# Eleven pairs of projection blocks as seven half-size products, convolution sums in PSUM, LayerNorm by token block

## The chip, the cores and the metric

The kernel runs on one core of a Trainium2 chip. Its metric is the device time of one execution in microseconds (us), the median of three runs. Five engines take part: TensorE (PE in the profile, its weight loads PEld), VectorE (DVE), ScalarE (ACT), GpSimd (POOL) and SyncE (SP), which issues most of the DMAs. Each engine takes its instructions strictly in the order in which they stand for it, so an instruction that waits holds up all that stand behind it on that engine.

## What is computed

One encoder layer over two batches (prompt and sample) of 512 tokens with 1024 channels, in fp32:

```python
h = rms_norm(x, norm_g)
c_q, c_kv, k_rope, gate_a, conv_in, gate_c, mg_a, mg_c = split_columns(h @ w_in)
attn = latent attention of 8 heads from c_q, c_kv and k_rope
y_a = (attn * silu(gate_a)) @ w_o_attn
u = conv_in[..., :1024] * sigmoid(conv_in[..., 1024:])
u = depthwise_conv(u, 31 taps) + dw_bias
u = silu(layer_norm(u, conv_ln_g, conv_ln_b)) * silu(gate_c)
y_c = u @ w_pw2
out = x + (sigmoid(mg_a) * y_a + sigmoid(mg_c) * y_c) @ w_out
```

## The kernel before, in words

**Layout.** The 1024 tokens of both batches lie along the free axis, channels on the 128 partitions. The normalized input h stands in SBUF as 8 slices of channels (k) by 2 batches (b), each 128x512. TensorE multiplies in fp32r, a format of reduced precision, so each operand is split into a high part and the remainder: `hH`, `hL` for h, `whi`, `wlo` for a weight block. A product is then the sum of three: high by high, low by high, high by low.

**Blocks.** The input projection runs in blocks of 128 output channels. One block (`block_mm`, L223) is 8 slices x 2 batches x 3 = 48 matmuls of 128x512 into one pair of PSUM banks. Each block's weights are loaded by SyncE (`load`, L108), rounded by ScalarE (`whi`, L124), and VectorE subtracts to get `wlo` (L125), two blocks ahead (`prep`, L128; `block`, L236). PSUM has three pairs of banks for blocks (pool `pp`) and two single banks (pool `p1`).

**Order of the blocks.** `cb` and `ca` are the gate and the value of the convolution input, `ma` and `mc` the merge gates, `ga` and `gc` the SiLU gates. For each of 8 groups of channels come `cb`, `ca` and two gate blocks; then four more gates and the eight `gc`. Finished `ma`, `mc` and `ga` gates are written out to DRAM (`gate_out`, L313).

**Convolution.** For each group the 31 taps run on all 1024 tokens at once: the first on ScalarE, with the bias (L250), the other 30 on VectorE, each reading and writing the same SBUF tile (L253):

```python
DVE.scalar_tensor_tensor(yt, u[:, :, i : i + S], dwk[:, j, i : i + 1], yt, op0=ALU.mult, op1=ALU.add)
```

`drain(n)` (L256) emits n taps between blocks and alternates between two groups when two are at hand.

**LayerNorm.** All eight convolved groups stay in SBUF. `ln_tok` (L348) transposes one block of 128 tokens to tokens-by-channels in PSUM, takes mean and variance and writes the normalized `z`; `swish` (L363) transposes one group of channels back, applies SiLU with gain and bias, multiplies by the `gc` gate and splits into `cH` and `cL`. Both are placed between the last gate blocks, each `swish` after a later block than its inputs. Then eight blocks multiply by `w_pw2` (`p`, L408), and latents, attention, output projection and the final product follow.

**Who sets the order.** A scheduler places the instructions on each engine: `tc.high_priority` draws some of them forward, `tc.manual_schedule` fixes a stretch at the start. Tiles of a pool rotate, and a tile's next use waits until its last readers are done.

Of the kernel before, what the change touches and what calls it, by code (L numbers as in the profile page):

```python
# [9 lines left out]
F32 = mybir.dt.float32  # L10
# [33 lines left out]
def encoder_block(tc, xp_d, xs_d, win_d, wkr_d, whd_d, wqr_d, wo_d, wp_d, wout_d, vec_d, dwk_d, rg_d, rc_d, yp_d, ys_d):  # L44
# [28 lines left out]
    wp = open_pool("w", bufs=2, side="left")  # L73
# [22 lines left out]
    spill = {"ma": ma_s, "mc": mc_s, "ga": ga_s}  # L96
# [10 lines left out]

    def load(i):  # L108
        src, n = wjobs[i]
        wraw[i] = wp.tile([P, D], F32, tag="raw", bufs=1, name=f"raw{i}")  # L110
        nc.sync.dma_start(wraw[i][:, :n], src)

    def split(i):
# [10 lines left out]
        nc.scalar.copy(hv, rv)  # L124
        DVE.tensor_sub(lv, rv, f(hv))  # L125
        wdone[i] = (hi, lo)

# [11 lines left out]
    others = [("ma", j) for j in range(6)] + [("mc", j) for j in range(KD)] + [("ga", j) for j in range(KD)]  # L139
    for j in range(KD):  # L140
        for key in [("cb", j), ("ca", j)] + others[2 * j : 2 * j + 2]:
            wjob(*key)
    late = others[2 * KD :]
    for key in late + [("gc", j) for j in range(KD)]:
        wjob(*key)
# [13 lines left out]
    for j in range(2):  # L159
        job(("w", j), wout_d[j])  # L160

# [41 lines left out]

    def evac_x(b, banks, ks):
        for k in ks:
            g = vec[:, V_NG + k : V_NG + k + 1]
            hi = hp.tile([P, S], F32R, name=f"hH{k}_{b}")
            lo = hp.tile([P, S], F32R, name=f"hL{k}_{b}")
            ACT(hi, banks[k], AF.Identity, scale=g)  # L209
            DVE.scalar_tensor_tensor(lo, banks[k], g, f(hi), op0=ALU.mult, op1=ALU.subtract)  # L210
            hH[k, b], hL[k, b] = hi, lo
# [29 lines left out]


# [4 lines left out]
    def conv_ops(j, u):  # L247
        yt = yp.tile([P, 2, S], F32, tag="y", name=f"y{j}")
        y[j] = yt
        ACT(yt, u[:, :, 0:S], AF.Identity, scale=dwk[:, j, 0:1], bias=vec[:, V_DB + j : V_DB + j + 1])  # L250
        yield
        for i in range(1, TAPS):
            DVE.scalar_tensor_tensor(yt, u[:, :, i : i + S], dwk[:, j, i : i + 1], yt, op0=ALU.mult, op1=ALU.add)  # L253
# [17 lines left out]
    load(1)  # L271
    banks = {}
# [6 lines left out]
    with tc.manual_schedule(engines={nc.scalar.engine, nc.vector.engine}):  # L279
# [5 lines left out]
        split(1)  # L285
        norm_x(1)
# [4 lines left out]
    for k in range(0, KD, 2):  # L291
        banks = {kk: x_bank(1, kk) for kk in (k, k + 1)}
        trans_x(1, banks, banks)
        evac_x(1, banks, banks)
    for i in (0, 1):
        block_mm(first[i], i, hh, hl, (1,))
        prep(i + 2)
        if i == 0:
            nc.sync.dma_start(dwk, dwk_d)
    DVE.tensor_mul(gqk, vec[:, V_GQ : V_GQ + 1], vec[:, V_GK : V_GK + 1])  # L300
    close_pool("x")
    yp = open_pool("y", bufs=8, side="left")
    sp = open_pool("s", bufs=9, side="left")
    cv = open_pool("cv", bufs=2, side="left")
    rg = cv.tile([P, 4, RD], F32, name="rg", bufs=1)
    rc = cv.tile([P, 2, 4, RD], F32, name="rc", bufs=1)
    nc.sync.dma_start(rg, rg_d)
    nc.sync.dma_start(rc, rc_d)

    def gate(nm, j, pool, tag):  # L310
        gate_out(nm, j, pool, tag, block(J[nm, j]))

    def gate_out(nm, j, pool, tag, ps):  # L313
        st = pool.tile([P, NT], F32, tag=tag, name=f"st{nm}{j}")
        ACT(st, ps, AF.Silu if nm == "ga" else AF.Sigmoid)
        nc.scalar.dma_start(spill[nm][j], st)

    for j in range(KD):
        ps = flat(first[0]) if j == 0 else block(J["cb", j])
        sig = cv.tile([P, NT], F32, tag="sig", name=f"sig{j}")  # L320
        ACT(sig, ps, AF.Sigmoid)
        drain(8)
        ps = flat(first[1]) if j == 0 else block(J["ca", j])
        u = cv.tile([P, 2, UW], F32, tag="u", name=f"u{j}", bufs=4)
        nc.gpsimd.memset(u[:, :, 0:PAD], 0.0)
        nc.gpsimd.memset(u[:, :, PAD + S : UW], 0.0)
        with tc.high_priority(offset=100):
            DVE.tensor_mul(u[:, :, PAD : PAD + S], half(ps), half(sig))
        waiting.append(conv_ops(j, u))
        drain(8)  # L330
        for key in others[2 * j : 2 * j + 2]:
            gate(*key, sp, "s")
            drain(8)
    for i in range(4):
        nc.gpsimd.tensor_mul(rt[:, i], rc[:, i % 2], rg[:, i].unsqueeze(1).to_broadcast([P, 4, RD]))


    sgc = {}
    z = {}
    cH = {}  # L340
    cL = {}

    def gate_c(j):
        ps = block(J["gc", j])
        sgc[j] = sp.tile([P, NT], F32, tag="s", name=f"sgc{j}")
        ACT(sgc[j], ps, AF.Silu)

    def ln_tok(i):  # L348
        ps = pp.tile([P, D], F32, tag="pp", name=f"yT{i}")
        for j in range(KD):  # L350
            nc.tensor.transpose(ps[:, j * P : (j + 1) * P], flat(y[j])[:, i * P : (i + 1) * P], identf)
# [8 lines left out]
        z[i] = zp.tile([P, D], F32, tag="z", name=f"z{i}", bufs=8)  # L360
        DVE.tensor_scalar(z[i], ps, mv[:, 0:1], rs, op0=ALU.subtract, op1=ALU.mult)

    def swish(j):  # L363
        ps = pp.tile([P, NT], F32, tag="pp", name=f"zT{j}")
        for i in range(8):
            nc.tensor.transpose(ps[:, i * P : (i + 1) * P], z[i][:, j * P : (j + 1) * P], identf)
        zs = zp.tile([P, NT], F32, tag="zs", name=f"zs{j}", bufs=2)
        ACT(zs, ps, AF.Silu, scale=vec[:, V_LG + j : V_LG + j + 1], bias=vec[:, V_LB + j : V_LB + j + 1])
        DVE.tensor_mul(zs, zs, sgc[j])
        cH[j] = yp.tile([P, NT], F32R, tag="y", name=f"cH{j}")  # L370
        cL[j] = sp.tile([P, NT], F32R, tag="s", name=f"cL{j}")
        nc.scalar.copy(cH[j], zs)
        DVE.tensor_sub(cL[j], zs, f(cH[j]))

    for key in late[:2]:
        gate(*key, sp, "s")
        drain(16)
    drain(1000)
    close_pool("cv")
    zp = open_pool("z", bufs=2, side="left")  # L380
    for n, key in enumerate(late[2:]):
        gate(*key, sp, "s")
        if n > 0:
            ln_tok(2 * n - 2)
            ln_tok(2 * n - 1)
    for j in range(KD):
        gate_c(j)
        if j == 0:
            ln_tok(6)
            ln_tok(7)  # L390
        else:
            swish(j - 1)
    swish(7)
    close_pool("z")

# [11 lines left out]
    for j in range(KD):  # L407
        ps = block(J["p", j], lambda k, b: cH[k][:, b * S : (b + 1) * S], lambda k, b: cL[k][:, b * S : (b + 1) * S])  # L408
# [4 lines left out]
    close_pool("m", "s", "y")  # L413
# [529 lines left out]
```

## Time and profile before

| what | value |
|---|---|
| median of 3 runs | 1188.58 us (1185.53 to 1188.98) |
| profiled execution, its own time | 1190.66 us |
| its span in the trace | 1188.9 us |
| PE busy | 1169.9 us, 98% of the span |
| DVE busy | 758.9 us, 64% |
| ACT busy | 399.6 us, 34% |
| POOL busy | 83.4 us, 7% |
| start of the first convolution tap | 50.70 us |
| start of the first LayerNorm transpose | 416.37 us |
| start of the first `p` block | 539.97 us |

The profile is one execution seen by the hardware profiler. Its views group instructions by line and shape (how often, busy time, mean duration), list them in order of time, give each engine's busy share in a stretch, and follow back the chain of work that ended last. "Idle before" is the time that the engine stood still ahead of an instruction, with what ended the wait.

### The profile page before, as it was taken

What the parts mean: (1) busy time and instruction counts of PE and PEld (TensorE: products, weight loads), DVE (VectorE), ACT (ScalarE), POOL (GpSimd) and SP (SyncE); (2) the same over time, 40 slices, a digit from 0 to 9 for tenths busy, and PEclk for the clock granted to TensorE, in tenths of its full rate; (3) what the DMA queues carried; (4) which work ended last, traced back from release to release, by engine and by line L of the source; (5) the groups of instructions that cost most, each with busy time, mean ns of one, the idle gap of its engine ahead of it and who ended that gap; (6) DMA issues with size and microseconds to landing.
All of it is one profiled execution on the core that took longest, in us unless ns stands there. A gap on an engine that the chain in (4) does not pass through costs nothing.

```text
span 1188.9 us, 14723 instructions
## 1 busy us (share of the span) xinstructions
PE 1169.9 (98%) x5988; PEld 992.2 (83%) x5988; DVE 758.9 (64%) x1094; ACT 399.6 (34%) x698; POOL 83.4 (7%) x108
## 2 busy tenths in 40 slices
PE   7999999999999999999999999999999999999998
PEld 5788888888888888888888887899999998888887
DVE  5599999999999854233121453777877889344411
ACT  5412211221122112332001335766676687122200
POOL 3000000000000000000000001322222221000000
PEclk9999999999999999999999999999999999999999
DMA  5122122212222321113442012011010112335432
GB/s 212 37 89 89 53 71 89 71 53 89 71 72 75 103 86 56 36 53 116 150 142 70 24 39 89 30 34 34 26 34 19 36 36 90 101 132 169 165 106 71
DMA packets 27571, 92.71 MB, mean 78 GB/s; under 512 B 3184, under 2 KB 3440, under 8 KB 27504
## 3 DMA queue, kind: packets, MB, share of 16 engines
q1 hardware_dynamic: 23760, 79.19, 19.8%
q10 hardware_dynamic: 3744, 12.58, 3.2%
q8 instruction: 47, 0.77, 0.3%
q14 instruction: 20, 0.16, 0.0%
HBM read 70.79 MB, written 20.97 MB: 77 GB/s over the span
## 4 chain that ended last, share of the span: by engine, by line
PE 94%; ACT 2%; DVE 1%; DMA 1%; POOL 1%; issue 0%; SPq 0%; ACTq 0%; DVEq 0%
PE blk L228 63%; PE po L865 7%; PE pt L632 2%; PE pkv L540 1%; PE pkv L542 1%; PE pkv L541 1%; PE av L642 1%; PE av L643 1%; PE av L644 1%; PE sc L613 1%; PE sc L615 1%; PE sc L614 1%; PE sc L616 1%; PE sc L617 1%; PE pq L569 1%; PE pq L570 1%
## 5 line engine op out<-in xcount | busy, mean ns | idle before, releaser
L228 PE MATMUL blk<-hH,whi 128*128 128x512 f32 x848 | 332.5, 393 | 1.6 <-ACT hH L209 0.7
L228 PE MATMUL blk<-hL,whi 128*128 128x512 f32 x848 | 332.6, 392 | 0.2 <-DVE hL L210 0.2
L253 DVE SCALAR_TENSOR_TENSOR y<-u,dwk,y 128x1024 f32<-128x1024 f32 x240 | 298.6, 1282 | 5.1 <-ACT y L250 1.4
L124 ACT CAST whi<-raw 128x1024 fp32r<-128x1024 f32 (+2 forms) x81 | 83.7, 1033 | 556.3 <-PE blk L228 540.9
L228 PE MATMUL blk<-hH,wlo 128*128 128x512 f32 x848 | 265.2, 391 | 0.3 <-DVE wlo L125 0.2
L228 PEld LDWEIGHTS blk<-hH,whi 128*128 128x128 f32 x848 | 160.0, 189 | 36.4 <-ACT hH L209 1.4
L228 PEld LDWEIGHTS blk<-hH,wlo 128*128 128x128 f32 x848 | 160.0, 189 | 34.1 <-DVE wlo L125 1.1
L228 PEld LDWEIGHTS blk<-hL,whi 128*128 128x128 f32 x848 | 160.1, 189 | 33.9 <-DVE hL L210 1.3
L125 DVE TENSOR_TENSOR wlo<-raw,whi 128x1024 fp32r<-128x1024 f32 (+1 forms) x80 | 96.9, 1211 | 126.6 <-ACT whi L124 126.6
L228 PE MATMUL blk<-a,whi 128*128 128x512 f32 x256 | 68.4, 389 | 0.0
L623 ACT ACTIVATE pr<-sc,nm,sqs 128x512 f32<-128x512 f32 x64 | 51.2, 800 | 28.0 <-DVE nm L621 28.0
L228 PEld LDWEIGHTS blk<-a,whi 128*128 128x128 f32 x256 | 48.0, 188 | 9.9
L410 DVE TENSOR_TENSOR tmc<-blk,smc 128x1024 f32<-128x1024 f32 x8 | 9.8, 1225 | 65.1 <-PE blk L228 65.1
L868 DVE TENSOR_TENSOR o<-po,xr 128x1024 f32<-128x1024 f32 (+1 forms) x9 | 10.0, 1106 | 64.1 <-PE po L865 64.1
L228 PE MATMUL blk<-cL,whi 128*128 128x512 f32 x128 | 49.8, 389 | 0.0
L228 PE MATMUL blk<-cH,whi 128*128 128x512 f32 x128 | 49.8, 390 | 0.0
L620 DVE TENSOR_REDUCE nm<-sc 128x1 f32<-128x512 f32 x64 | 43.7, 684 | 6.6 <-PE sc L617 6.4
L634 DVE TENSOR_TENSOR pt<-pt,pt 128x512 fp32r<-128x512 f32 x64 | 43.4, 682 | 1.0 <-ACT pt L633 0.8
L633 ACT CAST pt<-pt 128x512 fp32r<-128x512 f32 x64 | 38.8, 611 | 7.2 <-PE pt L632 7.1
L228 PE MATMUL blk<-a,wlo 128*128 128x512 f32 x128 | 39.4, 389 | 0.0
L228 PE MATMUL blk<-cH,wlo 128*128 128x512 f32 x128 | 39.4, 389 | 0.0
L632 PE MATMUL pt<-identf,pr 128*128 128x128 f32 x256 | 38.9, 275 | 0.0
(203 smaller groups left out, 1865.4 us busy)
## 6 DMA issues: line engine op xcount, KB each, us to landing
raw<-in_win_dram SPq DMA_DIRECT2D x53, 512.0 KB, 3.7
mc_s<-stmc ACTq DMA_DIRECT2D x8, 512.0 KB, 2.9
ga_s<-stga ACTq DMA_DIRECT2D x8, 512.0 KB, 3.3
raw<-in_wp_dram SPq DMA_DIRECT2D x8, 512.0 KB, 5.0
smc<-mc_s SPq DMA_DIRECT2D x8, 512.0 KB, 4.6
tc_s<-tmc SPq DMA_DIRECT2D x8, 512.0 KB, 2.9
sga<-ga_s SPq DMA_DIRECT2D x16, 256.0 KB, 2.6
raw<-in_wo_dram SPq DMA_DIRECT2D x8, 512.0 KB, 4.2
```

Of the source, the lines that this page charges most:

```text
L124: nc.scalar.copy(hv, rv)
L125: DVE.tensor_sub(lv, rv, f(hv))
L228: mm(ps[:, b], (wlo if wl_ else whi)[:, k], xl(k, b) if xl_ else xh(k, b), start=(k == 0 and wl_ == 0 and xl_ == 0), stop=(k == KD - 1 and ...
L253: DVE.scalar_tensor_tensor(yt, u[:, :, i : i + S], dwk[:, j, i : i + 1], yt, op0=ALU.mult, op1=ALU.add)
L540: mm(ps[:, t2], kh_, kh_w[:, k], start=(k == 0), stop=False)
L541: mm(ps[:, t2], kh_, kl_w[:, k], start=False, stop=False)
L620: DVE.reduce_max(nm, ps, axis=AX.X, negate=True)
L623: ACT(pr, ps, AF.Exp, bias=nm, scale=r["sq"][:, j : j + 1], accum_out=sm)
L632: nc.tensor.transpose(pt[:, kt], pr[:, kt * P : (kt + 1) * P], identf)
L633: nc.scalar.copy(pth[:, :, js], pt)
L634: DVE.tensor_sub(ptl[:, :, js], pt, f(pth[:, :, js]))
L865: mm(ps[:, n], lhs[k][:, ts_], w[k][:, n * S : (n + 1) * S], start=first_, stop=last_)
```

## The change

**Seven products for eight.** Of the blocks, 11 pairs are no longer two times 48 matmuls: `cb` with `ca` for the groups 2 to 7, the eight `gc` in four pairs, and `ga` 0 with 1. A pair is a 2x2 matrix (two blocks by two halves of the 1024 channels) times a 2x2 matrix (two halves by two batches), and is formed from 7 products of half depth with sums and differences before and after. A product has 12 matmuls, so a pair has 84. Sums of the weights (`s1` to `s4`) are made by GpSimd, sums of the input (`t1` to `t4`, and their parts `TH`, `TL`) once at the start by VectorE and GpSimd. After the products VectorE forms the outputs with five operations of 128x512 a pair (`u2`, `v`, and three sums in place in PSUM).

**Weights.** From the fifth block on, the low parts of weight blocks before LayerNorm's end are subtracted by GpSimd. Three raw and three split buffers stand where one and two stood.

**Convolution.** One group at a time; the running sum lies in a PSUM pair (`py`, which takes the two banks of `p1` until after the `p` blocks), the last tap writes to SBUF, and the group goes out to DRAM (`y_s`). The `gc` gates go to DRAM too (`gc_s`).

**LayerNorm.** Token block by token block: the block's 8 groups and its gate are loaded back from DRAM, transposed, normalized, transposed back, and finished, between the last six gate blocks. The weights of the first two `p` blocks are prepared after that.

The core of the diff:

```diff
+def sums(n, i1, i2):
+        s1, s2 = t(1), t(2)
+        nc.gpsimd.tensor_add(s1, r2[:, lo_], r2[:, hi_])
+        nc.gpsimd.tensor_add(s2, r1[:, lo_], s1)
...
+def ensure(m):
...
+                    split(i, nc.gpsimd if i >= 4 else None)
...
+                    for q, src in enumerate(sums(n, i1, i2)):
+                        nc.scalar.copy(hi[:, sl], src)
+                        nc.gpsimd.tensor_sub(lo[:, sl], src, f(hi[:, sl]))
...
+plan = [("cb", 0), ("ca", 0), ("cb", 1), ("ca", 1), ("ma", 0), ("ma", 1)]
...
+plan += twos + singles
+NLN = 6
...
+def combine_x(k, banks):
+        ACT(b22, banks[k + 4], AF.Identity, scale=g2)
+        DVE.scalar_tensor_tensor(t[1], banks[k], g1, xw[k], op0=ALU.mult, op1=ALU.subtract)
+        DVE.scalar_tensor_tensor(t[3], banks[k], g1, b22, op0=ALU.mult, op1=ALU.subtract)
+        nc.gpsimd.tensor_sub(t[2], b22, t[1])
+        nc.gpsimd.tensor_sub(t[4], xw[k + 4], t[2])
...
+        for n in (1, 3, 2, 4):
+            nc.scalar.copy(TH[n, k], t[n])
+            nc.gpsimd.tensor_sub(TL[n, k], t[n], f(TH[n, k]))
...
+def seven(emit):
...
+        product(a, e, 0, quad(0, 0), True)
+            nc.scalar.copy(p_a, a)
+        product(b, e, 1, comb(2), True)
+            DVE.tensor_sub(u2, p_a, b)
+        product(d, e + 1, 0, comb(3), True)
+        drain(2)
+        product(b, e + 1, 1, comb(1), False)
+            DVE.tensor_sub(v, p_a, b)
+            DVE.tensor_sub(b, d, v)
+        product(c, e + 2, 0, quad(1, 1), True)
+            DVE.tensor_add(c, c, v)
+        drain(3)
+        product(a, e + 2, 1, quad(1, 0), False)
+        emit(0, flat(px))
+        product(d, e + 3, 0, comb(4), False)
+            DVE.tensor_sub(d, d, u2)
+        drain(3)
+        emit(1, flat(py_))
...
 def conv_ops(j, u):
-            DVE.scalar_tensor_tensor(yt, u[:, :, i : i + S], dwk[:, j, i : i + 1], yt, op0=ALU.mult, op1=ALU.add)
+        yt = py.tile([P, 2, S], F32, tag="py", name=f"py{j}")
+            src = y[j] if i == 1 else yt
+            out = y[j] if i == TAPS - 1 else yt
+            DVE.scalar_tensor_tensor(out, u[:, :, i : i + S], dwk[:, j, i : i + 1], src, op0=ALU.mult, op1=ALU.add)
+        nc.sync.dma_start(y_s[j], flat(y[j]))
...
-            while len(active) < 2 and waiting:
+            while len(active) < 1 and waiting:
...
+    def load_tok(i):
+            nc.sync.dma_start(ytok[i], y_s[:, :, sl].rearrange("j p t -> p j t"))
+            nc.sync.dma_start(stok[i], gc_s[:, :, sl].rearrange("j p t -> p j t"))
...
+    def swish(i, z):
+        for j in range(KD):
+            ACT(zs[:, j], ps[:, j], AF.Silu, scale=vec[:, V_LG + j : V_LG + j + 1], bias=vec[:, V_LB + j : V_LB + j + 1])
...
+    close_pool("z", "s", "w1")
+    wp = open_pool("w", bufs=2, side="left")
+    prep(J["p", 0])
+    prep(J["p", 1])
```

**Where the instructions now stand.** On VectorE, in the middle of the convolution before the change: `y` of two groups, `u` the product of value and gate, `wlo` the low part of a weight block.

```order
L253 SCALAR_TENSOR_TENSOR y_982<-u_978,dwk,y_982 128x1024 [waits DVE_49] x7
L125 TENSOR_TENSOR wlo_1175<-raw_1172,whi_1174 128x1024 [waits DMAHW0_49,PE_49,Activation_49]
L253 SCALAR_TENSOR_TENSOR y_982<-u_978,dwk,y_982 128x1024 [waits DVE_49] x7
L328 TENSOR_TENSOR u_1242<-blk_1187,sig_1178 128x2x512 [waits PE_49,Activation_49]
L125 TENSOR_TENSOR wlo_1239<-raw_1236,whi_1238 128x1024 [waits DMAHW1_49,Activation_49]
L253 SCALAR_TENSOR_TENSOR y_982<-u_978,dwk,y_982 128x1024 [waits DVE_49]
L253 SCALAR_TENSOR_TENSOR y_1246<-u_1242,dwk,y_1246 128x1024 [waits Activation_49]
L253 SCALAR_TENSOR_TENSOR y_982<-u_978,dwk,y_982 128x1024 [waits DVE_49]
```

Nothing there but `u` waits for TensorE's current block, and nothing that TensorE's next matmuls need is made there but `wlo`. On the same engine after the change, one of the `gc` pairs late in the stage: `py` is the sum in PSUM, L373 writes `u2` (printed as u), L379 `v`, L380, L384 and L391 finish three of the four outputs in PSUM.

```order
L373 TENSOR_TENSOR u_2467<-pa_2466,blky_2465 128x512 [waits PE_49]
L409 SCALAR_TENSOR_TENSOR py_2458<-u_2160,dwk,py_2458 128x1024 [waits DVE_49] x5
L379 TENSOR_TENSOR v_2468<-pa_2466,blky_2465 128x512 [waits PE_49]
L409 SCALAR_TENSOR_TENSOR py_2458<-u_2160,dwk,py_2458 128x1024 [waits DVE_49]
L380 TENSOR_TENSOR blky_2465<-blky_2465,v_2468 128x512 [waits DVE_49]
L384 TENSOR_TENSOR blkx_2464<-blkx_2464,v_2468 128x512
L409 SCALAR_TENSOR_TENSOR py_2458<-u_2160,dwk,py_2458 128x1024 [waits DVE_49] x3
L391 TENSOR_TENSOR blky_2465<-blky_2465,u_2467 128x512 [waits PE_49]
L409 SCALAR_TENSOR_TENSOR py_2458<-u_2160,dwk,py_2458 128x1024 [waits DVE_49]
L409 SCALAR_TENSOR_TENSOR py_2458<-u_2160,dwk,py_2458 128x1024 [waits DVE_49,Pool_49]
L409 SCALAR_TENSOR_TENSOR py_2458<-u_2160,dwk,py_2458 128x1024 [waits DVE_49] x4
L373 TENSOR_TENSOR u_2616<-pa_2615,blky_2614 128x512 [waits PE_49,Activation_49]
```

TensorE's next products of a pair wait for these outputs, the taps stand between them, and each tap follows one that writes the same tile. On TensorE, LayerNorm's first place: before, `yT` is a transposed block of tokens.

```order
L351 MATMUL yT_2690<-identf,y_454 128x128 [waits Activation_49]
L351 MATMUL yT_2690<-identf,y_718 128x128
...
L351 MATMUL yT_2709<-identf,y_454 128x128 [waits Activation_49]
...
L228 MATMUL blk_2728<-hH_0_183,whi_2625 128x512
```

After the change, with `zT` the way back to channels and `blki` the next gate block:

```order
L528 MATMUL yT_3352<-identf,yt_3286 128x128 [waits DMAHW2_49,Activation_49]
L528 MATMUL yT_3352<-identf,yt_3286 128x128 x7
L528 MATMUL yT_3371<-identf,yt_3290 128x128 [waits DMAHW4_49,Activation_49]
L528 MATMUL yT_3371<-identf,yt_3290 128x128 x7
L544 MATMUL zT_3390<-identf,z_3369 128x128 [waits DVE_49,Activation_49]
L544 MATMUL zT_3390<-identf,z_3369 128x128 x7
L528 MATMUL yT_3415<-identf,yt_3411 128x128 [waits DMAHW6_49,PE_49]
L528 MATMUL yT_3415<-identf,yt_3411 128x128 x7
L325 MATMUL blki_3440<-hH_0_216,whi_3211 128x512 [waits DVE_49,PE_49]
```

The way back of the first token block, which needs VectorE's `z`, now stands right behind the second block's transposes and ahead of the next gate block.

More of the change, by code (lines that the diff above doesn't have):

```diff
@@ new lines, in encoder_block @@
+    take("cb", 0, flat(first[0]))
+    take("ca", 0, flat(first[1]))
+    for u in plan[2 : len(plan) - NLN]:
+        if isinstance(u[0], str):
+            take(*u, single())
+            drain(8)
+        else:
+            seven(lambda q, ps: take(*u[q], ps))
+            drain(6)
+    drain(1000)
+    close_pool("st", "y", "cv", "py")
+    close_pool("hT")
+    cp2 = open_pool("c", bufs=1, side="right")
+    cH = [cp2.tile([P, KD, S], F32R, name=f"cH{b}") for b in range(2)]
+    cL = [cp2.tile([P, KD, S], F32R, name=f"cL{b}") for b in range(2)]
@@ L307, in encoder_block @@
+    zp = open_pool("z", bufs=2, side="left")
+    rg = zp.tile([P, 4, RD], F32, name="rg", bufs=1)
+    rc = zp.tile([P, 2, 4, RD], F32, name="rc", bufs=1)
     nc.sync.dma_start(rg, rg_d)
     nc.sync.dma_start(rc, rc_d)
[L310 to L333, printed above, removed]
@@ L359, in ln_tok @@
         rsqrt(rs, rs)
[L360 to L394, printed above, removed]
+        z = zp.tile([P, D], F32, tag="z", name=f"z{i}")
```

224 lines of the change are left out of this document (188 added, 36 removed).

## The prediction

> **What bounds the kernel now.** I read the page's busy shares first, then the chain that ended last, then the busy time by stretches of the span, and last the groups of instructions and single engines in order of time. The shares:
>
> ```profile
> PE 1169.9 (98%) x5988; PEld 992.2 (83%) x5988; DVE 758.9 (64%) x1094; ACT 399.6 (34%) x698; POOL 83.4 (7%) x108
> ```
>
> The chain (start, length, what) and three stretches (length, then busy time and count of PE, PEld, DVE, ACT, POOL, then PE's granted clock):
>
> ```profile
> 47.05 369.32 PE blk L228 x1628
> ```
>
> ```profile
> 100.00:200.00 100.00, 100.00 (x443) 82.80 (x442) 93.58 (x77) 20.08 (x20) 0.54 (x6) 1.00 0.23 74
> ```
>
> ```profile
> 47.05:416.37 369.32, 369.32 (x1630) 305.78 (x1631) 344.87 (x282) 72.55 (x71) 0.72 (x8) 1.00 0.24 77
> 416.37:539.97 123.60, 123.60 (x610) 103.56 (x607) 49.72 (x63) 34.31 (x35) 4.26 (x8) 1.00 0.17 56
> ```
>
> TensorE is the bound: nothing else lies on the chain for 369 us, at full granted clock. But VectorE is a close second there, busy 344.87 of 369.32 us, 93%. The page's 64% hides that. A change that takes work from TensorE in this stage has only 7% before VectorE is the bound.
>
> One matmul of 128x512 costs 100/443 = 0.2257 us, a block of 48 costs 10.83 us, a pair of blocks 21.67 us, and a pair of 84 matmuls 18.96 us.
>
> **What TensorE saves.** 11 pairs times 12 matmuls are 132 fewer, at 0.2257: **-29.8 us**. The number of LayerNorm transposes stays at 128.
>
> **What VectorE has to do in the stage of the pairs.** Taps before, first by group, then in order of time (start, length):
>
> ```profile
> L253 DVE SCALAR_TENSOR_TENSOR y<-u,dwk,y 128x1024 f32<-128x1024 f32 x240 | 298.6, 1282 | 5.1 <-ACT y L250 1.4
> ```
>
> ```profile
> 53.03 6.56 DVE L253 SCALAR_TENSOR_TENSOR y<-u,dwk,y 128x1024 f32<-128x1024 f32 x5
> 59.51 1.22 DVE L125 TENSOR_TENSOR wlo<-raw,whi 128x1024 fp32r<-128x1024 f32 x1
> 60.65 9.20 DVE L253 SCALAR_TENSOR_TENSOR y<-u,dwk,y 128x1024 f32<-128x1024 f32 x7
> ...
> 309.96 9.65 DVE L253 SCALAR_TENSOR_TENSOR y<-u,dwk,y 128x1024 f32<-128x1024 f32 x8
> ```
>
> At 60.65 only one group is at hand, so each tap waits for the one before it: (9.20 - 1.28) / 6 = 1.32 us from start to start. At 309.96 two groups alternate: (9.65 - 1.28) / 7 = 1.196 us. The difference of 0.124 us is what the dependence costs. A tap followed by something else takes 59.51 - 53.03 - 4 x 1.32 = 1.20 us, and a two-operand 128x1024 operation 60.65 - 59.51 = 1.14 us. After the change one group runs at a time, so the dependent price is back everywhere. A 128x512 operation comes from LayerNorm's statistics, four in a row up to the next start: (420.58 - 418.18) / 4 = 0.60 us.
>
> ```profile
> 418.18 2.48 DVE L356 BATCH_NORM_STATS2 bst<-yT 128x6 f32<-128x512 f32 x4
> 420.58 0.32 DVE L357 BATCH_NORM_AGGREGATE mv<-bst 128x2 f32<-128x12 f32 x2
> 420.82 0.27 DVE L358 TENSOR_SCALAR lrs<-mv 128x1 f32<-128x1 f32 x2
> 421.69 2.60 DVE L361 TENSOR_SCALAR z<-yT,mv,lrs 128x1024 f32<-128x1024 f32 x2 [0.59 <-POOL lrs L178]
> ```
>
> In the new order VectorE has, from the first `u2` (L373) to the last sum into `c` (L384), 149 taps followed by a tap, 48 followed by something else, 53 half operations and 6 products `u`: 149 x 1.32 + 48 x 1.20 + 53 x 0.60 + 6 x 1.14 = 292.9 us. TensorE has between the same points 1188 matmuls, 268.1 us. VectorE issues in order, `u2` and `v` stand behind taps, and the next products need the PSUM banks that these operations finish. So the longer one sets the pace: 292.9 + 0.7 (the last sum itself and its hand-over) - 268.1 = **+25.7 us**. For a pair that follows a pair, with 15 taps (11 followed by a tap) and 5 halves, this is 22.3 us against 18.96. The weights' `wlo` no longer stand on VectorE there; without their move it would be worse. Behind the last pair only 11 taps are left beside seven blocks (about 70 us), so the end of the convolution costs nothing.
>
> **The unknown in that price: a tap that reads and writes its sum in PSUM.** No row of before writes PSUM from VectorE. The nearest that read it:
>
> ```profile
> L410 DVE TENSOR_TENSOR tmc<-blk,smc 128x1024 f32<-128x1024 f32 x8 | 9.8, 1225 | 65.1 <-PE blk L228 65.1
> L369 DVE TENSOR_TENSOR zs<-zs,sgc 128x1024 f32<-128x1024 f32 x8 | 9.7, 1225 | 5.6 <-ACT zs L368 5.6
> L361 DVE TENSOR_SCALAR z<-yT,mv,lrs 128x1024 f32<-128x1024 f32 x8 | 10.4, 1340 | 2.3 <-POOL lrs L178 2.3
> ```
>
> L410 reads PSUM and L369 does not: 1225 ns both. So I take the old 1282. Bounds: 1225 (-57 ns on 197 taps, -11.2 us) and 1340, L361, which reads PSUM with two per-partition operands (+58 ns, +11.4 us). The dependence could also vanish, 149 x 0.124 = -18.5 us, for a result may be seen sooner in PSUM. Each 0.01 us on a tap is 2.0 us on the kernel while VectorE sets the pace.
>
> [...]
>
> **GpSimd's share.** Its rate on such tiles:
>
> ```profile
> L564 POOL TENSOR_TENSOR kk<-krs,kk 128x512 fp32r<-128x512 f32 x16 | 20.5, 1284 | 40.2 <-ACT kk L562 40.2
> ```
>
> A pair needs 4 sums and 7 low parts: 11 x 1.284 = 14.1 us, under the 18.96, so nothing is added while no other engine stretches these operations.
>
> **The start.** The first gates wait for the sums of the input:
>
> ```profile
> 30.32 1.27 ACT L209 ACTIVATE hH<-xT,vec 128x512 fp32r<-128x512 f32 x2 [3.28 <-PE xT L202]
> ...
> 45.76 1.28 ACT L321 ACT_TABLE_LOAD   x1
> 47.05 1.02 ACT L321 ACTIVATE sig<-blk 128x1024 f32<-128x1024 f32 x1
> ```
>
> ```profile
> L210 DVE SCALAR_TENSOR_TENSOR hL<-xT,vec,hH 128x512 fp32r<-128x512 f32 x16 | 11.6, 748 | 10.9 <-ACT hH L209 10.8
> L605 ACT CAST k<-pkr 128x512 fp32r<-128x512 f32 x16 | 9.8, 613 | 0.0
> L124 ACT CAST whi<-raw 128x1024 fp32r<-128x1024 f32 x71 | 74.7, 1053 | 523.9 <-PE blk L228 518.1 <-PE blk L699 3.4 <-PE pq L570 2.3
> ```
>
> From 30.32, one more weight cast (1.05), the activation (0.64), `t[1]` and `t[3]` (0.75 each), a cast (0.61) and 0.4 of hand-overs put GpSimd's first `TL` at 34.5. ScalarE's cast of the last combined slice stands ahead of the first sigmoid and waits for GpSimd's 20th operation: 34.5 + 20 x 1.284 = 60.2. Then cast 0.61, table load 1.28, sigmoid 1.02: 63.1. That sigmoid frees the PSUM pair for the fourth block, which before started 44 matmuls after 47.05, at 57.0. TensorE waits **+6.0 us**; 3 if some of the 20 fall ahead of the wait, 10 if GpSimd is a sixth slower.
>
> **LayerNorm.** Transposes of before, 16 in one piece of the chain, and one row for a 128x128 activation:
>
> ```profile
> 416.37 1.75 PE yT L351 x16
> ```
>
> ```profile
> 989.03 1.14 ACT L579 ACTIVATE ks<-pkv,rk 128x128 f32<-128x128 f32 x4
> ```
>
> Eight transposes take 0.87 us. At the first place `zT` stands right behind the second block's transposes. Before, the first `z` was done at 421.69 + 1.30 = 422.99, 4.8 us after the transposes began to be read; it can begin one block (0.87) earlier: TensorE waits 4.0. At the next three places TensorE has 3 x 0.87 = 2.6 us of transposes, while ScalarE has sigmoid 1.02, table load 1.28 and eight activations (a little under 1.14 / 4 each as they overlap, 2.1) before the pair of banks comes free: 4.4 - 2.6 = 1.8 each, 5.4. At the last place `zT` waits for `z` of the block just transposed: statistics 1.20, 0.16, 0.13, GpSimd's root 0.6, `z` 1.30, less one other `zT`: 2.5. The first `p` block waits for a weight cast that stands behind the last gate's sigmoid, 1.02 + 1.05, and then for `wlo`, 1.22 less four matmuls: 2.4. Together 14.3. Before, the stretch from 416.37 lost 123.6 - 10 x 10.83 - 16 x 0.87 = 1.3 to the same. So **+13.0 us**, with nothing else to cover it, since all else waits for TensorE; 6 if the scheduler's hand-overs overlap better. The reloads of tokens (8 + 8 of 512 KB) lie a block ahead on SyncE, whose queue holds only weights for later blocks behind them: nothing.
>
> **The sum.** 1190.7 (the profiled execution's own time) + 6.0 - 29.8 + 25.7 + 13.0 = 1205.6; that execution lies 2.1 above the median of its runs, so the forecast is **1203.5 us**.
>
> **The rivals.**
>
> *Taps in PSUM are cheaper and TensorE stays the bound.* If a dependent tap costs 1.20 or less, VectorE's 292.9 falls by 149 x 0.12 = 17.9 and with a duration nearer to L410's by up to 11.2 more: the 25.7 are gone, 1203.5 - 25.7 = **1178 us**. From a price 0.076 us lower on (14.9 us / 197) the change is a gain. For it speaks L410's 1225; against it, that the 0.124 are seen on this very operation. This is the rival on the other side.
>
> *Taps in PSUM are dearer*, as L361: 1203.5 + 11.4 = **1215 us**.
>
> *GpSimd is stretched by VectorE.* The same tiny operation, alone and beside a VectorE run:
>
> ```profile
> 26.13 0.55 POOL L178 TENSOR_TENSOR rr<-rr,mhalf 128x1 f32<-128x1 f32 x1 [0.63 <-DVE rr L191]
> 27.31 1.30 POOL L178 TENSOR_TENSOR rr<-rr,mhalf 128x1 f32<-128x1 f32 x1 [0.64 <-DVE rr L191]
> ```
>
> ```profile
> 27.16 2.74 DVE L197 TENSOR_SCALAR xt<-xt,rr 128x1024 f32<-128x1024 f32 x4
> ```
>
> It took 0.75 us longer there. On all 20 operations at the start this is +15: **1218 us**. In the pairs 11 x 2.03 = 22.4 us would only equal VectorE's 22.3. Against it: at the start VectorE is idle most of the time. [...]
>
> *Start and LayerNorm are hidden*, VectorE being the bound as forecast: 1203.5 - 6.0 - 13.0 = **1184.5 us**. Against it: the new order puts each waiting instruction directly ahead of TensorE's next block.
>
> **How the numbers follow.** Forecast 0.44 (own range 1190 to 1213: tap at L410's duration 1192, the start 3 to 10, LayerNorm 6 to 13), cheaper taps 0.30, dearer taps 0.11, start and LayerNorm hidden 0.08, GpSimd stretched 0.07. Cheaper taps at 1178 less half of what LayerNorm adds give the low end, 1174; the high end, 1220, takes in the dearer taps and the stretched GpSimd. A measurement can tell 0.3%, 3.6 us, from no change. Faster by more: cheaper taps (0.27 of their 0.30) and 0.05 of the hidden start, 0.32. Within: 0.03 + 0.03 + 0.05 of the forecast's lower part, 0.11. Slower: 0.57.
>
> **What would show it.** In the changed kernel's profile: the taps at L409, 1282 ns and 1.32 from start to start (right), or near 1.20 (the first rival); idle time of TensorE ahead of the products L353 to L355, ended by VectorE, about 2.3 us a pair; the first sigmoid at about 62 and TensorE's wait behind it; 128x512 rows of GpSimd near 1284 ns, or near 2000; idle time of TensorE at `zT` and behind it, about 14 us between the first transpose (416.37 before) and the first `p` block. The forecast is wrong if TensorE shows no wait in the pairs, or if its matmuls are no longer 0.2257 apart.

## The result, and the profile after

The changed kernel takes 1245.68 us (median of 4 runs, 1243.87 to 1251.86), the kernel before beside it 1187.05: a ratio of 1.0503, 95% interval 1.0460 to 1.0546. The forecast was 1203.5 us and at most 1220. The direction was right; the loss over before was some four times the forecast.

The page's shares of the changed kernel (its profiled execution took 1251.86 us, span 1250.1):

```profile
PE 1171.0 (94%) x5856; PEld 976.2 (78%) x5856; DVE 772.4 (62%) x1115; ACT 479.3 (38%) x860; POOL 330.7 (26%) x281
```

TensorE has 132 matmuls fewer and is busy as long as before. The stages: the pairs (from the first `u2` to the last sum into `c`), the single blocks behind them, LayerNorm (columns as in the prediction):

```profile
102.00:417.10 315.10, 281.77 (x1168) 219.07 (x1166) 292.73 (x257) 95.05 (x125) 161.11 (x128) 0.98 0.24 81
427.50:498.50 71.00, 71.00 (x316) 58.76 (x315) 15.49 (x13) 15.60 (x16) 20.57 (x12) 1.00 0.50 161
498.50:598.20 99.70, 77.89 (x368) 64.76 (x366) 42.23 (x57) 53.71 (x92) 11.36 (x11) 0.91 0.33 102
```

VectorE is busy 292.73 us in the pairs, forecast 292.9. But the stretch lasts 315.1, so even VectorE idles there, 7%.

The forecast counted 1188 matmuls between the same points; the row has 1168, because the scheduler put some of the last pair's products behind them (the trace has all 5856 of the kernel's matmuls, 5988 less 132). They are worth 1168 x 0.2257 = 263.6 us, so 51.5 are lost. (By the code's count of 1188 it is 47.0, the figure that some expectations below use.) Of the 51.5 us 33.3 are idle. The other 18.2 are mostly restarts: from 152.45 to 153.70 in the rows below two matmuls take 1.25 us, 0.53 of them idle and 0.45 their usual time, so a wait costs some 0.27 us beyond its idle time. Most of the rest is a lower rate behind three of the waits (last section).

What TensorE waited for in the pairs, up to 407 us (in all, times, longest), then in LayerNorm:

```profile
PE blkx L355 <- POOL olo L179: 11.0, 14, 1.4
PE blkx L353 <- ACT ohi L178: 7.4, 14, 0.5
PE blky L353 <- DVE u L373: 6.4, 6, 1.9
PE blki L325 <- ACT whi L128: 2.9, 3, 1.0
PE blki L325 <- POOL wlo L129: 2.5, 2, 1.3
```

```profile
PE blki L325 <- ACT zs L547: 9.4, 3, 3.5
PE zT L544 <- DVE z L538: 7.2, 2, 4.1
PE blk L325 <- ACT whi L128: 2.6, 1, 2.6
PE zT L544 <- ACT stmc L473: 1.3, 1, 1.3
PE yT L528 <- ACT stmc L473: 1.3, 1, 1.3
```

In the pairs most waits are short, and they end with weight parts (`ohi`, `olo`), not with VectorE. One of them on ScalarE and on TensorE:

```profile
152.69 0.62 ACT L178 CAST ohi<-raw 128x512 fp32r<-128x512 f32 x1 [7.54 <-PE blky L354]
```

```profile
152.45 0.39 PE L355 MATMUL blky<-tH,olo 128*128 128x512 f32 x1
153.37 0.50 PE L353 MATMUL blkx<-hH,ohi 128*128 128x512 f32 x1 [0.53 <-ACT ohi L178]
153.70 0.40 PE L354 MATMUL blkx<-hL,ohi 128*128 128x512 f32 x1
154.73 0.50 PE L355 MATMUL blkx<-hH,olo 128*128 128x512 f32 x1 [0.63 <-POOL olo L179]
```

ScalarE had stood still for 7.54 us. It cast as soon as TensorE's product `b'` had freed the weight tile, and TensorE's next product was the one that needed this cast. The order on TensorE, here where a pair follows a pair, shows why. `blkx` holds a and c, `blky` d and b; the number behind `ohi` is the weight tile of the pair (0: a, b; 1: d, b'; 2: c, a'; 3: d'), and only each product's first row is shown:

```
L353 MATMUL blkx_1294<-hH_0_216,ohi_0_1216 128x512 [waits Activation_49]
...
L353 MATMUL blky_1143<-tH_0_373,ohi_3_1181 128x512 [waits DVE_49]
...
L353 MATMUL blkx_1142<-hH_0_232,ohi_2_1147 128x512 [waits DVE_49]
...
L353 MATMUL blkx_1294<-hH_1_359,ohi_2_1299 128x512 [waits Activation_49]
...
L353 MATMUL blky_1295<-tH_0_128,ohi_0_1216 128x512 [waits Activation_49]
...
L353 MATMUL blky_1295<-tH_0_132,ohi_1_1258 128x512 [waits DVE_49]
```

The code has a, b, d, b', c, a', d'. The scheduler runs a, then the previous pair's d' and a', then c, b, d and b'. So c comes ahead of b, and d, ahead of which `u2` must be ready, directly behind b. Seven of the eleven pairs follow a pair; the trace has one wait for `u2` and two places with a wait for weight parts (`ohi`, then `olo`) for each of the seven (the last `u2` at 408.35, behind the window of the table).

### The profile page after: what moved, and what is told of

Its sections match the earlier page's. It is cut to its first block, busy times and chain, and to the rows that moved or that the text cites. A ratio compares the mean times of both kernels' runs of the same rounds, so it can differ in the third digit from the quotient of the medians.

```text
span 1250.1 us, 14992 instructions
## 1 busy us (share of the span) xinstructions
PE 1171.0 (94%) x5856; PEld 976.2 (78%) x5856; DVE 772.4 (62%) x1115; ACT 479.3 (38%) x860; POOL 330.7 (26%) x281
## 4 chain that ended last, share of the span: by engine, by line
PE 61%; ACT 3%; DVE 1%; POOL 1%; issue 0%; ACTq 0%; DVEq 0%; POOLq 0%
PE blk L325 20%; PE blki L325 11%; PE po L1052 7%; PE pt L819 2%; PE pkv L727 1%; PE pkv L728 1%; PE pkv L729 1%; PE av L829 1%; PE av L830 1%; PE av L831 1%; PE sc L803 1%; PE sc L800 1%; PE sc L802 1%; PE sc L801 1%; PE sc L804 1%; PE pq L756 1%
## 5 line engine op out<-in xcount | busy, mean ns | idle before, releaser
L409 DVE SCALAR_TENSOR_TENSOR py<-u,dwk,py 128x1024 f32<-128x1024 f32 x224 | 288.6, 1288 | 6.7
L128 ACT CAST whi<-raw 128x1024 fp32r<-128x1024 f32 (+3 forms) x59 | 60.4, 1024 | 320.7 <-PE blk L325 166.3
L325 PE MATMUL blki<-hH,whi 128*128 128x512 f32 x352 | 141.3, 401 | 14.9 <-ACT zs L547 9.4
L325 PE MATMUL blki<-hL,whi 128*128 128x512 f32 x352 | 139.9, 398 | 0.0
L325 PE MATMUL blki<-hH,wlo 128*128 128x512 f32 x352 | 111.3, 397 | 4.2 <-POOL wlo L129 3.8
L325 PEld LDWEIGHTS blki<-hH,whi 128*128 128x128 f32 x352 | 68.2, 194 | 31.9 <-ACT zs L547 10.1
L179 POOL TENSOR_TENSOR olo<-s,ohi 128x512 fp32r<-128x512 f32 x44 | 58.7, 1345 | 75.9 <-ACT ohi L178 75.9
L353 PE MATMUL blky<-tH,ohi 128*128 128x512 f32 x176 | 70.2, 399 | 7.7 <-DVE u L373 7.2
L355 PE MATMUL blky<-tH,olo 128*128 128x512 f32 x176 | 69.2, 393 | 0.0
L354 PE MATMUL blky<-tL,ohi 128*128 128x512 f32 x176 | 69.1, 393 | 0.0
L325 PE MATMUL blk<-hH,whi 128*128 128x512 f32 x144 | 57.9, 408 | 0.9 <-ACT hH L306 0.7
L325 PE MATMUL blk<-hL,whi 128*128 128x512 f32 x144 | 58.2, 404 | 0.2 <-DVE hL L307 0.2
```

The costliest lines, as they stand in the source:

```text
L179: nc.gpsimd.tensor_sub(lo[:, sl], src, f(hi[:, sl]))
L325: mm(ps[:, b], (wlo if wl_ else whi)[:, k], xl(k, b) if xl_ else xh(k, b), start=(k == 0 and wl_ == 0 and xl_ == 0), stop=(k == KD - 1 and ...
L353: mm(ps, hi[:, k], xh, start=first and k == 0, stop=False, skip_group_check=not first)
L354: mm(ps, hi[:, k], xl, start=False, stop=False, skip_group_check=not first)
L355: mm(ps, lo[:, k], xh, start=False, stop=k == 3, skip_group_check=not first)
L409: DVE.scalar_tensor_tensor(out, u[:, :, i : i + S], dwk[:, j, i : i + 1], src, op0=ALU.mult, op1=ALU.add)
```

## The experiments

Each ratio is to the kernel before on the same chip, with its 95% interval. That kernel's medians went from 1187.05 to 1190.08 us, so a difference of up to some 3 us between two of the kernels below is not settled.

**Half the taps.** In `conv_ops`:

```diff
+            if i % 2 == 0 and i != TAPS - 1:
+                yield
+                continue
```

> Leaves out 14 of each group's 30 VectorE taps (the even ones but the last), in the same places of the order, so the convolution is not computed in full; everything else stays. In the changed kernel VectorE is busy 292.7 of the 315.1 us between the first u2 and the last sum into c, and TensorE has 268.1 us of matmuls there. Theory A (VectorE's taps set the pace of the pairs): 112 taps of 1.3 us go, TensorE becomes the bound, and the stretch falls by 30 to 45 us: 1200 to 1215 us. Theory B (weights set the pace: of TensorE's idle time in that stretch 23.8 us end with ScalarE's or GpSimd's weight parts, 6.8 us with VectorE): only those 6.8 us go, 1235 to 1240 us. Both in part: about 1220 us, with the weights' waits of some 20 us still in the trace.

1240.25 us, 1.0433 (1.0415 to 1.0452): 5 us less. The stretch with VectorE at little more than half:

```profile
102.00:417.00 315.00, 286.84 (x1202) 226.72 (x1201) 176.36 (x165) 98.55 (x128) 164.14 (x130) 0.98 0.25 86
```

TensorE still idles for 28 us. Theory A, the forecast's own, falls. The waits for weight parts did not stay at 18.4 us either: leaving out taps changes what the scheduler lays out, and 9.0 were left, with 9.5 us behind the sigmoids of three pairs in their place. The time lies 0.25 us above B's range; its reason came out only in part.

**A fourth weight buffer.** In `split` and `ensure`, every fourth weight tile from a pool of its own:

```diff
+        q = wx if wx is not None and len(made) % 4 == 3 and len(made) < len(stream) - NLN else wp
-        hi = wp.tile([P, D], F32R, tag="whi", name=f"whi{i}")
+        hi = q.tile([P, D], F32R, tag="whi", name=f"whi{i}")
```

> A fourth buffer for the split weights (high and low part) in the stage of the pairs; to make room the rotary tables are made behind LayerNorm. Nothing is left out. Theory B (TensorE waits because a cast can begin only when the third buffer back is free, directly ahead of its use): the waits on ScalarE's and GpSimd's weight parts, 23.8 us, go almost wholly, and the time falls by 15 to 22 us to 1224 to 1230 us. Theory A (VectorE sets the pace): TensorE waits for VectorE in their place, at most 5 us are gained: 1240 us or more, with TensorE's idle time ended by VectorE risen from 6.8 to about 25 us.

1225.01 us, 1.0304 (1.0286 to 1.0321): 20.7 us less, as B has it.

**No pairs.**

```diff
     plan += twos + singles
+    plan = [k for u in plan for k in ([u] if isinstance(u[0], str) else list(u))]
```

> No pair is formed from seven products: every block is 48 matmuls again; taps in PSUM, one group at a time, 8 to a block, weights on GpSimd and LayerNorm by token block stay as in the changed kernel. 132 more matmuls are 29.8 us. Theory A: 8 taps take 10.6 us beside a block of 10.83, so VectorE no longer holds TensorE and the 47 us lost in the pairs go: 1246 + 29.8 - 47 = about 1228 us. Theory B: a block's weights are needed as closely as before, 10 to 20 us of waits remain: 1238 to 1250 us. If the loss does not come from the pairs at all: 1275 us.

1226.80 us, 1.0315 (1.0300 to 1.0331). TensorE was busy in all 315 us of the old stretch. So without any pair the change costs 37 us (start and LayerNorm), and the eleven pairs, which take away 29.8 us of matmuls, make the kernel 19 us longer instead. A's number came out, but at eight taps a block nothing there tells VectorE from the order of the products.

**SiLU gates at the end.**

```diff
-    singles = [("ga", j) for j in range(2, KD)] + [("ma", j) for j in range(2, 6)] + [("mc", j) for j in range(KD)]
+    singles = [("ma", j) for j in range(2, 6)] + [("mc", j) for j in range(KD)] + [("ga", j) for j in range(2, KD)]
```

> The six gate blocks that stand between the token blocks of LayerNorm are ga gates (SiLU, as LayerNorm's own activation) in place of mc gates (sigmoid), so that ScalarE loads no activation table there; the order of the gates is all that changes. Theory L1 (ScalarE's chain of weight cast, table load, gate, table load and eight activations of 0.35 us is what TensorE waits for at three places): 2.6 us less at two places and 1.3 to 2.6 at the third and at the last, 7 to 12 us faster: 1234 to 1239 us. Theory L2 (the stage is slow by its granted clock of 0.91 and by waits for z, which do not depend on tables): less than 3 us faster.

1234.81 us, 1.0385 (1.0364 to 1.0407): 10.9 us less, within L1's range.

**Four buffers and half the taps**, both edits as above.

> Four split buffers and, of each group's 30 VectorE taps, 14 left out (the convolution is not computed in full). With three buffers leaving out the taps gave 5 us, with all taps the fourth buffer gave 21 us, and with it TensorE still loses about 28 us to the pairs (1225.0 us, of which 37.3 us over before are seen without any pair). Theory A2 (once the weights come in time, VectorE's 293 us of work set the pace, the term of the forecast): the time falls by 20 to 28 us to 1197 to 1205 us. Theory C (each pair loses by its hand-overs on ScalarE: copies, gates and casts that wait in order): it falls by less than 8 us, 1217 us or more.

1222.89 us, 1.0285 (1.0248 to 1.0322): 2.1 us less than with all taps, no more than the noise. A2 falls. With VectorE busy 177 us of the 315, the waits in the pairs are:

```profile
PE blky L355 <- DVE u L375: 5.7, 5, 1.5
PE blkx L355 <- ACT ohi L180: 4.8, 9, 0.6
PE blkx L357 <- POOL olo L181: 3.1, 5, 0.6
PE blky L355 <- DVE blky L382: 2.1, 3, 0.9
```

The fourth buffer did not end the waits for weight parts: 7.9 us are left. As much, 7.8 us, ends with VectorE, although it has less to do. That it begins only when TensorE is already waiting fits this, but this run alone does not show it.

**LayerNorm staggered**, with four buffers and SiLU gates at the end; `l` is a token block's transposes and `z`, `s` the way back, one list behind each gate block, and a token block's reload follows its transposes:

```diff
-    NLN = 6
+    NLN = 9
+    steps = [["l0", "l1"], ["s0", "l2"], ["s1", "l3"], ["s2", "l4"], ["s3", "l5"], ["s4", "l6"], ["s5", "s6", "l7"], ["s7"], []]
```

> Four split buffers; ga gates (SiLU) and three mc gates as the last nine blocks; and LayerNorm staggered: a token block goes back to channels only behind the next gate block, so that nothing TensorE needs is made directly ahead of it. Nothing is left out. Theory L1 (LayerNorm's 30 us are waits of TensorE for a chain directly ahead of it, the lower clock following from them): 22 to 28 us less than with four buffers alone, 1197 to 1203 us, and a granted clock of 1.0 in that stage. Theory L2 (the stage's clock and reloads from DRAM set its time): 1210 us or more.

1207.52 us, 1.0157 (1.0126 to 1.0187): 17.5 us less, between L1 and L2. TensorE now came to LayerNorm so early that it waited 8.8 us for the reload of a group whose convolution had just ended; without that it would be L1's number, which no run shows.

**The same without pairs.**

> No pairs (every block 48 matmuls), the late gates and the staggered LayerNorm as in the run beside it. By L1 1226.8 - 25 = 1202 us. With the pairs and four buffers 28 of the 29.8 us that they save are lost again, so the two should come out within 4 us of each other; if the pairs are a clear gain by now, this one is slower by more than 8 us.

1203.19 us, 1.0119 (1.0084 to 1.0154): 23.6 us less than the other kernel without pairs. It is 4.3 less than the kernel with pairs, but the two intervals overlap. The granted clock of its profiled execution is 1.00. L1 holds.

**Four taps a group off VectorE**, in the staggered kernel with pairs. `ahead` does the first four taps of the groups 1 to 7, one group early:

```diff
+            ACT(tmp, u[:, :, i : i + S], AF.Identity, scale=dwk[:, j, i : i + 1])
+            nc.gpsimd.tensor_add(y[j], y[j], tmp)
```

> As the kernel with four buffers and staggered LayerNorm, and of the groups 1 to 7 four taps each leave VectorE: ScalarE multiplies, GpSimd adds, one group ahead. VectorE is relieved of 28 x 1.32 = 37 us. Theory A2 (VectorE sets the pace of the pairs once the weights come in time): 18 to 26 us less than without it, 1174 to 1184 us, faster than before the change. Theory C: no gain, or a loss where the additions (28 x 2.4 us on GpSimd) delay the weights.

1204.80 us, 1.0133 (1.0106 to 1.0159): 2.7 us less, with overlapping intervals. A2 fails a second time.

**The products in another order**, in the changed kernel; the weights are made in that order too, and the taps' places between the products move along:

```diff
-            stream += [(n, i, i + 1) for n in range(4)]
+            stream += [(n, i, i + 1) for n in (0, 2, 1, 3)]
...
-        product(d, e + 1, 0, comb(3), True)
+        product(c, e + 1, 0, quad(1, 1), True)
         drain(2)
-        product(b, e + 1, 1, comb(1), False)
+        product(a, e + 1, 1, quad(1, 0), False)
+        ensure(e + 5)
+        product(d, e + 2, 0, comb(3), True)
+        drain(3)
+        product(b, e + 2, 1, comb(1), False)
...
-        product(c, e + 2, 0, quad(1, 1), True)
...
-        drain(3)
-        product(a, e + 2, 1, quad(1, 0), False)
```

> The changed kernel with one thing moved: the seven products of a pair stand as a, b, c, a', d, b', d', and their weights are made in that order, so that c and a' (5.4 us) lie between b and the products that wait for u2, and each weight tile is used by two products in a row. Three split buffers and all taps stay. Theory C (TensorE loses by what is made directly ahead of its use: weights that were needed out of their order, and u2): most of the 18.4 us of waits for weight parts of the pairs and the 7.2 us for u2 go, 15 to 25 us faster: 1221 to 1231 us. Theory A (VectorE's 293 us): VectorE is left as busy, at most 5 us: 1241 us or more. If the number of buffers and not the order is the cause: less than 8 us.

1202.93 us, 1.0105 (1.0088 to 1.0122): 42.8 us less than the changed kernel, far beyond what any theory gave. The same stretch:

```profile
102.00:417.10 315.10, 315.10 (x1387) 259.46 (x1386) 295.51 (x261) 107.81 (x137) 172.67 (x134) 1.00 0.29 99
```

TensorE is never idle, with VectorE at 295.51 us as before and the same three weight buffers.

**The order of products alone**, the weights made in the old order:

> The changed kernel with the products of a pair in the order a, b, c, a', d, b', d', but with their weights still made in the old order, so that c and a' use the third weight tile ahead of the second. Theory W (weights needed out of the order in which they are made are what TensorE waited for): the waits for weight parts stay, 12 to 18 us, only u2's 7 us go: 1225 to 1238 us. Theory H (what counts is that c and a' lie between b and the products that wait for u2 and v): 1203 to 1210 us, as with both moved.

1206.46 us, 1.0147 (1.0130 to 1.0165): theory H. In its trace no wait for weight parts is left in the pairs. The cast that stood directly ahead of its product now starts two products early, when a' frees a tile:

```profile
148.10 0.62 ACT L178 CAST ohi<-raw 128x512 fp32r<-128x512 f32 x1 [4.82 <-PE blkx L354]
```

**Everything together**: the order of products, four buffers, staggered LayerNorm and four taps off VectorE; then with the first sigmoid drawn forward (`tc.high_priority(offset=1500)` around the first two `take`); then with the fourth block's low part on GpSimd (`i >= 3` for `i >= 4`).

> The order of products a, b, c, a', d, b', d' in the kernel with four split buffers, staggered LayerNorm and four taps a group on ScalarE and GpSimd (1204.8 us). Theory C: of its 14 us of waits in the pairs 8 to 12 go, and the half rate behind the longer ones: 1190 to 1197 us. If VectorE set the pace there, no gain: 1202 us or more.

1186.14 us (10 runs, 1175.96 to 1187.79), 0.9944 (0.9916 to 0.9971): faster than before the change, and below the range that theory C gave.

> As the kernel beside it, with the first sigmoid drawn ahead of ScalarE's cast that waits for GpSimd's sum of the input. If that cast holds TensorE (the 1.8 us ahead of the fourth block) the kernel gains 2 to 3 us against the one beside it; if the sums hold TensorE elsewhere, nothing.

1180.85 us (1177.76 to 1186.07), 0.9922 (0.9892 to 0.9952), the lowest median of all. The two sets of times overlap, so the 2 to 3 us are not settled. TensorE waited 10.4 us for the sigmoid in the profiled execution of the kernel beside it (1187.79 us) and 2.5 us in this one's (1177.76 us), but that difference does not lie in the cast that the edit moved: in the profile of the kernel beside it this cast took 0.61 us and waited for nothing. In both, VectorE's `wlo`, then a load of weights, then ScalarE's cast of them come ahead of the sigmoid; first the kernel beside it, then this one:

```profile
55.82 8.78 DVE L130 TENSOR_TENSOR wlo<-raw,whi 128x1024 fp32r<-128x1024 f32 x1 [1.33 <-ACT whi L129]
68.11 0.62 ACT L180 CAST ohi<-raw 128x512 fp32r<-128x512 f32 x1 [10.34 <-DMA raw<-in_win_dram]
```

```profile
55.02 1.46 DVE L130 TENSOR_TENSOR wlo<-raw,whi 128x1024 fp32r<-128x1024 f32 x1 [1.36 <-ACT whi L129]
59.98 0.62 ACT L180 CAST ohi<-raw 128x512 fp32r<-128x512 f32 x1 [3.01 <-DMA raw<-in_win_dram]
```

SyncE issued that load at 64.63 and at 56.52, each time as soon as `wlo` had let go of the raw weights, so the 8.78 us of `wlo` (last section) delayed the sigmoid. Behind the first 100 us of the one and the first 90 of the other, both executions take 1086 us.

> The fastest kernel so far (1180.9 us, runs of 1177.8 to 1186.1) with the low part of the fourth block's weights on GpSimd in place of VectorE, where it took 8.8 us in seven of the runs before it, locked out from its start to the first gap in GpSimd's row of operations. If that lock-out makes the spread of the runs at the start, all runs come near the low end: 1175 to 1180 us. If the spread comes from elsewhere, the median stays at 1180 to 1184 us.

1183.88 us (6 runs, 1181.64 to 1186.35), 0.9952 (0.9935 to 0.9969): no gain. The lock-out was not gone, it had moved to the first tap (last section). Whether the times of the runs that were not profiled spread by the same chain stays open, and so does the share of each edit in the sum: the new order with the staggered LayerNorm alone was not run.

## Why the prediction was wrong

**The matmuls.** 132 fewer at 0.2257 us: right, -29.8 (the traces have 5988 and 5856); with the order mended TensorE shows 0.2272 (315.10 / 1387 recorded).

**VectorE's work.** Right to the microsecond: 292.73 busy, 292.9 forecast, though partly by terms that cancel. The seven first taps, which read their sum from SBUF, took 1718 ns on average, 3.0 us more than forecast in all. The taps with their sum in PSUM:

```profile
L409 DVE SCALAR_TENSOR_TENSOR py<-u,dwk,py 128x1024 f32<-128x1024 f32 x224 | 288.6, 1288 | 6.7
```

```profile
77.89 23.87 DVE L409 SCALAR_TENSOR_TENSOR py<-u,dwk,py 128x1024 f32<-128x1024 f32 x18
```

1288 ns each, (23.87 - 1.29) / 17 = 1.33 us from start to start. The two rivals on the price of a tap are both out: 1288 against 1282 ns. GpSimd's 128x512 rows took 1345 ns (`olo`) and not 2000, so that rival is out as well; and the start and LayerNorm were not hidden, as the next terms show.

**The step that failed** is "So the longer one sets the pace: ... = +25.7 us" (its own terms add up to 25.5). Pace was the wrong measure. GpSimd's share, "so nothing is added", rests on the same comparison of sums, and 18.4 us of TensorE's waits ended with the weight parts `ohi` and `olo`. TensorE needs from VectorE only five short operations a pair, and `u` in six pairs, not the taps; the taps may fall behind, since the blocks after the pairs need nothing of them. Nor, in the main, did the taps hold up `u2`:

```profile
L373 DVE TENSOR_TENSOR u<-pa,blky 128x512 f32<-128x512 f32 x11 | 7.5, 686 | 8.7 <-PE blky L355 8.7
```

In nine of the eleven pairs VectorE stood idle, 8.7 us in all, until TensorE's product b was there. TensorE in turn waited 7.2 us for `u2`, 0.7 a pair where the forecast's sign was 2.3. How much room there was shows in the first LayerNorm row of the changed kernel:

```profile
499.40 2.49 DVE L533 BATCH_NORM_STATS2 bst<-yT 128x6 f32<-128x512 f32 x4 [56.06 <-PE yT L528]
```

VectorE had been done for 56 us. In the kernel with the new order the last tap starts at 436.57 (442.06 in the changed kernel), so VectorE hardly changes, while the first transpose starts at 449.6, not at 498.5. What cost the 51.5 us was, nearly all of it, the order: where a pair follows a pair, each of a, c and d stood directly behind the product that freed its weight tile or on which its `u2` waited. A wait of about 1 us each, with a restart behind it, and the lower rate behind some. Moving c and a' between b and d returned 42.8 us: in the same stretch some 2 us were then lost (315.1 less 1387 x 0.2257), and 4.8 came back as a wait for reloaded tokens, as LayerNorm began earlier. TensorE's order as built held the clue; the prediction read VectorE's order for the pairs, and TensorE's only for LayerNorm.

**LayerNorm.** Forecast 14.3 us of waits, measured 21.8; with the matmuls at 240 x 0.2257 + 128 x 0.109 = 68.2, the 99.7 us lost 31.5. The first place was right (4.0 forecast, 4.1 measured), the last (2.5 against 3.1) and the first `p` block (2.4 against 2.6) nearly so. At the places between, the forecast had gate, one table load and eight activations, 4.4 us. The trace:

```profile
519.69 1.06 ACT L128 CAST whi<-raw 128x1024 fp32r<-128x1024 f32 x1 [8.13 <-PE blki L325]
520.76 1.28 ACT L473 ACT_TABLE_LOAD   x1
522.06 1.02 ACT L473 ACTIVATE stmc<-blki 128x1024 f32<-128x1024 f32 x1
523.10 1.28 ACT L547 ACT_TABLE_LOAD   x1
...
544.87 2.90 ACT L547 ACTIVATE zs<-zT,vec 128x128 f32<-128x128 f32 x8
```

A weight cast and a second table load stand ahead of the gate, and eight activations take 2.90, not 2.1: 7.5 us in a row, so 9.4 + 2.6 us of waits for 5.4. The SiLU gates took 10.9 us of this away. The other 9.7 us of the 31.5 are restarts and slow matmuls, which the forecast did not have.

**The start.** Forecast 6.0. TensorE's matmuls in the first 100 us, before and after:

```profile
0.00:50.00 50.00, 40.53 (x177) 30.68 (x178) 23.75 (x41) 26.85 (x39) 9.19 (x26) 1.00 0.37 137
50.00:100.00 50.00, 50.00 (x222) 41.40 (x221) 47.57 (x39) 9.88 (x10) 0.00 (x0) 1.00 0.23 74
```

```profile
0.00:50.00 50.00, 38.01 (x161) 27.52 (x162) 28.26 (x46) 30.66 (x49) 33.01 (x35) 1.00 0.40 150
50.00:100.00 50.00, 47.78 (x210) 38.95 (x209) 42.84 (x28) 18.62 (x24) 33.03 (x30) 1.00 0.14 51
```

399 against 371: 28 x 0.2257 = 6.3 us. The first sigmoid started at 61.71, forecast about 62: it stood on ScalarE behind a cast that waited 2.25 us for GpSimd's `t` and began at 59.78, though TensorE had ended the sigmoid's own block by 55.13. The fourth block behind it started at 62.79, forecast 63.1. But TensorE came to that block at 61.0, not at 57.0 as forecast, so the wait there was 1.8 us. The rest was lost ahead of it, largely in short waits that the forecast did not have; that 6.0 and 6.3 agree so closely is partly luck.

**The sum in the two profiled executions**, 61.2 us of span: 6.3 - 29.8 + 51.5 + 30.2 (31.5 less the 1.3 that before lost) + 3.0 behind LayerNorm = 61.2. With the order of products mended the kernel takes 1202.9, the forecast's number by other terms, which is luck.

## What to carry to other kernels

When two engines exchange small results and one may run ahead, the larger busy sum need not set the pace; look at each exchange for what stands between the producer's start and the consumer's first instruction, in the order as built. Half the load taken from a suspected engine is a cheap test of such a bound, and here it refuted one whose work had been forecast to the microsecond. Put independent products between a product and the one that waits for its result, and give LayerNorm's way back a block's distance from its input.

## What the hardware showed beyond this

**Half rate after a wait.** Behind the 1.88 us that TensorE waited for `u2`, in the changed kernel:

```profile
171.82 0.50 PE L353 MATMUL blky<-tH,ohi 128*128 128x512 f32 x1 [1.88 <-DVE u L373]
...
173.18 0.63 PE L354 MATMUL blky<-tL,ohi 128*128 128x512 f32 x1
173.61 0.63 PE L355 MATMUL blky<-tH,olo 128*128 128x512 f32 x1
174.04 0.63 PE L353 MATMUL blky<-tH,ohi 128*128 128x512 f32 x1
...
176.73 0.40 PE L355 MATMUL blky<-tH,olo 128*128 128x512 f32 x1
176.96 0.39 PE L353 MATMUL blky<-tH,ohi 128*128 128x512 f32 x1
```

From start to start 0.43 us in place of 0.23, for about 3.3 us; the granted clock was 0.59 from 171.8 to 175.2 and 1.00 from 176 to 180. A wait of 4.1 us in LayerNorm was followed by some 6 us at this rate, waits of 0.5 us by none. The length alone does not decide: in the same execution waits of 1.27 us (at 206.27) and 1.42 us (at 260.63), each with a shorter one some 2 us ahead of it, were followed by about 3 us at this rate, while a wait of 1.37 us (at 353.88) after such a shorter one, and one of 2.70 us in LayerNorm (at 565.92), were not. The longest wait in the pairs was 1.9 us; what decides which waits the half rate follows was not shown.

**GpSimd locks VectorE out.** A VectorE operation that reads two SBUF tiles, while GpSimd works without a gap:

```profile
55.58 8.81 DVE L129 TENSOR_TENSOR wlo<-raw,whi 128x1024 fp32r<-128x1024 f32 x1 [1.33 <-ACT whi L128]
```

```profile
55.95 2.55 POOL L299 TENSOR_TENSOR tL<-t,tH 128x512 fp32r<-128x512 f32 x2
58.45 1.29 POOL L293 TENSOR_TENSOR t<-b,t 128x512 f32<-128x512 f32 x1
59.70 2.38 POOL L129 TENSOR_TENSOR wlo<-raw,whi 128x1024 fp32r<-128x1024 f32 x1
62.03 1.28 POOL L299 TENSOR_TENSOR tL<-t,tH 128x512 fp32r<-128x512 f32 x1
63.24 0.13 POOL L484 MEMSET u<- 128x30 f32 x1
```

It takes 1.22 us alone and 8.8 here, and ends at 64.39, about its own duration behind the end of GpSimd's row of additions (63.31). In the last kernel of the experiments that low part was gone, and the first tap of the convolution, which reads its sum from SBUF, took 8.79 us in its place. The prediction had this only the other way round (a GpSimd operation of 0.55 us that took 1.30 beside VectorE). Taps with one input in SBUF ran beside GpSimd at 1288 ns. In these rows VectorE was kept out over a whole row of GpSimd's instructions: this low part took 8.77 to 8.82 us in eight profiled kernels that have it there. In a ninth, the one with the first sigmoid drawn forward, it got in behind the first of them and took 1.46 us. What decides this stays open.
